# The last filter's xm in another buffer, and the Fourier stage's subtractions from GpSimd to VectorE

## The chip, the cores and the metric

The kernel runs on one core of one Trainium2 chip. A core has several engines that work side by side: TensorE (matmuls), VectorE, ScalarE, GpSimd, and SyncE (SP), which here only starts DMA transfers. Each engine takes its instructions in the order in which they were written into its own stream, and waits there where a semaphore says that an operand or a buffer isn't ready. In the rows of the profile they are called PE, DVE, ACT, POOL and SP. The metric is the device time of one execution in microseconds, as the median over runs. Lower is better.

## The reference

One encoder layer is computed for two sequences (prompt and sample) of 1024 rows by 1024 channels, in float32. Cut to what matters:

```python
xn = rmsnorm(x, g_pre)
p = xn @ w_in                                    # 1024 x 8192
fv, fg, hv, hg, mg = split(p)
fz = fftn(fv, axes=(row, within a group of 256), norm="ortho").real
y_f = (fz * silu(fg)) @ w_fourier_out
v, x1, x2 = split(short_conv(hv, w_short))       # width 3, each channel
kf = hyena_filters(...)                          # 2 x 1024 filters, as spectra
z = v
for n, gate in enumerate((x1, x2)):
    z = gate * (irfft(rfft(z, 2L) * kf[:, n])[:L] + hyena_d[n] * z)
y_h = (z * silu(hg)) @ w_hyena_out
g_f, g_h = split(sigmoid(mg + b_merge))
y = x + rmsnorm((g_f * y_f + g_h * y_h) @ w_out, g_post)
```

The filters depend on no input sequence, so they are made once and serve both.

## The kernel before, in words

Every float32 operand of a large matmul is split into two halves, a high one (h) and a low one (l = value - h). `split` makes h on ScalarE (a cast) and l by a subtraction on the engine that its argument names. `mm3` then issues three matmuls (h·h, h·l, l·h) for each product. Names ending in h and l in the rows are these halves.

**The Fourier stage** takes about the first 245 us. The first sequence goes through `first_half`, with `two_weights` for its first weights. For the second sequence, `xtile` (L427 to L451) is called for each of eight tiles k of 128 channels. It loads `xk`, scales and transposes it on TensorE (`tpx`) into `xg`, adds and subtracts the two mirrored halves of `xg` into the even and odd part of `eo`, and splits `eo` into `eh` and `el`. `weights` (L458 to L468) does the like for a slice `wfv` of the weights: sum `wer`, difference `wor`, and their halves `we` and `wo`. The matmuls `pfv` multiply both; `pse`, `pso`, `pP` and `pQ` make the transforms behind them, and VectorE's `sst`, `pp`, `qp`, `fA` and `fB` work on those.

**The filter stage** (`phase_main`, about 245 to 700 us) makes 16 filters. `filter_taps` (L737) makes a filter's taps: matmuls `pft` from the hidden layer `hid`, an exponential `ex` on ScalarE, the products `T` and sums of their absolute values `acc` on VectorE, and then the matmul `pn`, which sums over partitions. `filter_spectrum` (L774) takes `T` and `pn`'s reciprocal `invn`, forms the sums `fE` and `fO`, from these `xp` and `xm`, and hands both to `butterfly` (L659), which leaves them in `b`, `bs`, `bh` and `bl`. `forward` turns these by the matmuls `pXf` into a spectrum, which is stored as `kt`. Between the filters stand the large projection matmuls `pin` (`inproj`), which need nothing of the filters, and so fill TensorE's time. The projection's own weights `wr` are loaded by SP, and their low half `wl` is a subtraction on GpSimd, here and in the whole kernel. The hidden layer is loaded from memory as `hidr` at the stage's start.

**The branches** (about 670 to 1667 us) begin with `conv(1, 0)`: the projection `pin`, ScalarE's scaled copy into `v` (L873), and two VectorE steps on `v` (L874, L875). `conv_front` (L896) makes `eo4` from it (written `eo` in the rows) and transposes that on TensorE (`tph`). After the branches come three output products.

**Buffers.** A tile is taken by its tag from a pool; with `bufs=1` the next tile of that tag waits until the last reader of the one before is done. `Rooms` sends a tag to one of two pools: "q", with two buffers, is in the first, and "u", with one, in the second. `xp` takes "q". `xm` takes "u", and so does `v`, which is the only output of `conv` that does.

**The order of work** isn't written out by hand. A scheduler works with its own model of times on the whole program, and sets the order in each engine's stream once, before the program runs. An edit at one place can thus move rows at others.

Of the kernel before, what the change touches and what calls it, by code (L numbers as in the profile page):

```python
# [9 lines left out]
F32 = mybir.dt.float32  # L10
# [6 lines left out]
P = 128  # L17
# [143 lines left out]
class K:  # L161
# [265 lines left out]
    def xtile(self, b, k, px, fo):  # L427


        nc, a = self.nc, self.a  # L430
        xt = px.tile([P, 8, P], F32, tag="x", name=f"xk{b}_{k}", bufs=3)
        nc.sync.dma_start(xt.rearrange("p m c -> p (m c)"), a["x1c"][k])
        xg = px.tile([P, L + 2], F32, tag="xg", name=f"xg{b}_{k}", bufs=2)
        nc.gpsimd.memset(xg[:, L:L + 2], 0.0)
        for n in range(2):
            tp = self.psum("mm", 4, "tpx")
            for q in range(4):
                m = 4 * n + q
                self.mm(tp[:, q * P:(q + 1) * P], xt[:, m], self.diag[:, m], True, True)
            nc.scalar.activation(xg[:, 512 * n:512 * n + 512], tp, AF.Copy, scale=self.gpre[:, k:k + 1])  # L440
        nc.sync.dma_start(self.d_x[b][k], xg[:, 0:L])
        eo = px.tile([P, 2, 2, 256], F32, tag="eo", name="eo", bufs=2)
        fw = xg[:, 0:512].rearrange("p (a r) -> p r a", r=2)
        bw = xg[:, 1024:512:-1].rearrange("p (a r) -> p r a", r=2)
        self.add("dve", eo[:, 0], fw, bw)
        self.sub("pool", eo[:, 1], fw, bw)
        self.split(fo["eh"][:, k], fo["el"][:, k], eo, "dve", "act")
        x5 = fo["x5"][:, k]
        hi = x5[:, b:b + 33:32]
        nc.scalar.copy(hi, xg[:, 512:513].to_broadcast([P, 2]))  # L450
        nc.scalar.activation(x5[:, 2 + b:35 + b:32], hi.bitcast(F32), AF.Identity, bias=xg[:, 512:513], scale=-1.0)  # L451
# [6 lines left out]
    def weights(self, pw, W, half, k):  # L458

        nc, a = self.nc, self.a  # L460
        w = pw.tile([P, 2, 2, 130], F32, tag="wfv", name="wfv", bufs=2)
        nc.sync.dma_start(w.rearrange("p a b c -> p (a b c)"), a["w_fv"][k * P:(k + 1) * P, half])
        we = pw.tile([P, 2, 130], F32, tag="wer", name="wer", bufs=2)
        wo = pw.tile([P, 2, 128], F32, tag="wor", name="wor", bufs=2)
        self.add("dve", we, w[:, :, 0], w[:, :, 1])
        self.sub("pool", wo, w[:, :, 0, 0:128], w[:, :, 1, 0:128])
        for r, t in ((we, W[0]), (wo, W[1])):
            self.split(t[0][:, k], t[1][:, k], r.rearrange("p a b -> p (a b)"), "pool" if r is wo else "dve", "act")  # L468

    def mm3(self, out, L_, R_, start, stop):  # L470

# [302 lines left out]
    def filter_spectrum(self, n, ct, T, ws):  # L774
        nc = self.nc
        E = ws.tile([P, 4, 2, P], F32, tag="t4", name="fE", bufs=2)
        O = ws.tile([P, 4, 2, P], F32, tag="t4", name="fO", bufs=2)
        for h, t in enumerate(T):
            self.add("dve", E[:, 2 * h:2 * h + 2], t[:, :, 0], t[:, :, 1])
            self.sub("dve", O[:, 2 * h:2 * h + 2], t[:, :, 0], t[:, :, 1])  # L780
        xp = ws.tile([P, 2, 4, P], F32, tag="q", name="xp", bufs=2)
        xm = ws.tile([P, 2, 4, P], F32, tag="u", name="xm", bufs=1)
        self.add("dve", xp[:, 0], E[:, :, 0], E[:, ::-1, 1])
        self.sub("dve", xm[:, 0], E[:, :, 0], E[:, ::-1, 1])
        self.sub("dve", xp[:, 1], O[:, :, 0], O[:, ::-1, 1])
        self.add("dve", xm[:, 1], O[:, :, 0], O[:, ::-1, 1])
        B = self.butterfly(ws, xp, xm)
        for g, pairs in GROUPS:
            X = self.forward(g, pairs, B[g], "pXf")
            kt = ws.tile([P, 8, P], F32, tag="k", name="kt", bufs=2)  # L790
            tmp = ws.tile([P, 2, 2, P], F32, tag="tt", name="ktmp", bufs=4)
            th = lambda j: self.th[:, 6 * pairs[0] + j:6 * pairs[0] + j + 1]
            if g:

                nc.scalar.activation(tmp, X, AF.Copy, scale=th(0))
                self.stt("dve", kt[:, 0:6:5], X[:, :, 1], th(1), tmp[:, :, 0])
                self.stt("dve", kt[:, 2], X[:, 1, 0], th(4), tmp[:, 1, 1])
                self.stt("dve", kt[:, 4], X[:, 0, 0], th(1), tmp[:, 0, 1], MUL, SUB)
                self.turned = nc.scalar.mul(kt[:, 1:4:2], kt[:, 0:4:2], -1.0)
            else:  # L800
                for i, pr in enumerate(pairs):
                    R, I = X[:, i, 0], X[:, i, 1]
                    th = lambda j: self.th[:, 6 * pr + j:6 * pr + j + 1]
                    nc.scalar.activation(tmp[:, i, 0], R, AF.Copy, scale=th(0))
                    nc.scalar.activation(tmp[:, i, 1], R, AF.Copy, scale=th(3))
                    self.stt("dve", kt[:, 2 * i], I, th(1), tmp[:, i, 0])
                    self.stt("dve", kt[:, 4 + i], I, th(2), tmp[:, i, 1])
                    if i == 0:
                        t2 = ws.tile([P, P], F32, tag="y", name="kt2", bufs=1)
                        nc.scalar.activation(t2, R, AF.Copy, scale=th(4))  # L810
                        self.stt("dve", kt[:, 1], I, th(5), t2)
                    else:
                        nc.scalar.mul(kt[:, 3], kt[:, 2], -1.0)
            o = KOFF[g] * P
            dk = self.d_k[n][ct][:, o:o + 8 * P].rearrange("p (a b) -> p a b", a=8)
            nc.sync.dma_start(dk[:, 0:4], kt[:, 0:4])
            for r in range(2):
                nc.sync.dma_start(dk[:, 4 + r::2], kt[:, 4:6])
# [902 lines left out]
```

## Time and profile before

| what | value |
|---|---|
| runs | 2364.63, 2364.76, 2366.9 us, median 2364.76 |
| profiled execution, its own time | 2366.49 us |
| its span, first to last instruction | 2364.7 us |
| mean granted TensorE clock | 0.996 |
| busy: TensorE, VectorE, ScalarE, GpSimd | 2322.0, 1968.6, 1117.0, 449.8 us |

Of these 449.8 us on GpSimd, 51.4 lie in subtractions of the Fourier stage's weights and tiles. The times that follow are counted from the start of the span of the profiled execution, and so lie 1.8 us below its own time. A row of a timeline reads: start, duration, engine, line, operation, written tile <- read tiles, shapes, count, and in brackets how long the engine had stood idle, and on whom it had waited. A row of groups has the count, then busy time and mean ns of one, then the idle time before them. A row of the list of waits has total, number, and longest.

### The profile page before, as it was taken

To read this page: it belongs to the slowest core of one execution; us is meant where nothing else is said; L and a number is where in the kernel's file an instruction comes from. 1 tells how busy PE (TensorE), PEld (TensorE's weight loads), DVE (VectorE), ACT (ScalarE), POOL (GpSimd) and SP (SyncE) were. 2 spreads that over 40 slices of the span, in tenths; PEclk is the share of its full clock that TensorE was granted. 3 is DMA by queue.
4 is the path that set the end of the run, shared out by engine and by line. 5 is a ranking of instruction groups with operands and counts; after the bars stand their busy time and mean duration, and the time that the engine had idled before them with its cause. 6 is when DMAs were issued, how large, how long until landed. Compare 5 with 4: busy or idle time off the path is not lost.

```text
span 2364.7 us, 36212 instructions
## 1 busy us (share of the span) xinstructions
PE 2322.0 (98%) x12784; PEld 2019.3 (85%) x12784; DVE 1968.6 (83%) x3438; ACT 1117.0 (47%) x2080; POOL 449.8 (19%) x428
## 2 busy tenths in 40 slices
PE   6999999999999999999999999999999999999998
PEld 5999888888888888888888889888888888888787
DVE  7775688888788999999989989997765578777987
ACT  6654576777753333334222223323443364557443
POOL 3342222122223343321000000112000000101311
PEclk9999999999999999999999999999999999999999
DMA  7636765554565667667465554445854678998653
GB/s 263 210 141 215 267 211 177 180 168 155 183 219 201 194 207 216 207 198 248 165 205 167 175 171 157 159 152 194 313 167 146 218 260 269 271 312 245 199 165 142
DMA packets 246207, 479.69 MB, mean 203 GB/s; under 512 B 24582, under 2 KB 82280, under 8 KB 245706
## 3 DMA queue, kind: packets, MB, share of 16 engines
q1 hardware_dynamic: 222013, 402.25, 50.9%
q0 software_dynamic: 23792, 75.11, 11.2%
q8 instruction: 100, 1.64, 0.3%
q14 instruction: 81, 0.66, 0.1%
q10 hardware_dynamic: 221, 0.04, 0.0%
HBM read 326.82 MB, written 177.73 MB: 213 GB/s over the span
## 4 chain that ended last, share of the span: by engine, by line
PE 55%; DVE 2%; DMA 1%; ACT 1%; issue 1%; POOL 0%; DVEq 0%; POOLq 0%; ACTq 0%; SPq 0%
PE pin L194 18%; PE pg L194 15%; PE pn L194 12%; PE pT L194 5%; PE pX L194 5%; PE tph L906 1%; DMA x<-d_x 1%; DMA xr<-in_x 0%; DMA d_m<-gt 0%; DMA k<-d_k 0%; DVE x L177 0%; DVE wl L181 0%; DVE t L181 0%; DVE wraw L181 0%; ACT room L171 0%
## 5 line engine op out<-in xcount | busy, mean ns | idle before, releaser
L194 PE MATMUL pin<-x,wh 128*128 128x512 f32 x2816 | 891.5, 392 | 0.6 <-DVE x L177 0.6
L194 PEld LDWEIGHTS pin<-x,wh 128*128 128x128 f32 x2816 | 525.3, 189 | 100.7 <-ACT v L873 0.8
L194 PE MATMUL pin<-x,wl 128*128 128x512 f32 x1408 | 552.1, 392 | 0.0
L181 POOL TENSOR_TENSOR wl<-wr,wh 128x512 fp32r<-128x512 f32 x128 | 224.6, 1755 | 709.7 <-ACT wh L171 682.0
L194 PEld LDWEIGHTS pin<-x,wl 128*128 128x128 f32 x1408 | 265.6, 189 | 50.0
L194 PE MATMUL pn<-room,wh 128*128 128x512 f32 x864 | 266.1, 389 | 0.0
L194 PEld LDWEIGHTS pn<-room,wh 128*128 128x128 f32 x864 | 162.1, 188 | 33.6 <-DVE gt L181 0.2
L194 PE MATMUL pn<-room,wl 128*128 128x512 f32 x432 | 168.4, 390 | 0.1
L181 DVE TENSOR_TENSOR t<-pX,k 128x1024 f32<-128x1024 f32 x128 | 156.2, 1220 | 8.7 <-PE pX L194 7.4
L194 PE MATMUL pX<-bh,cfwd 128*128 128x256 f32 x768 | 161.3, 288 | 0.0
L194 PE MATMUL pT<-cinv,yh 128*128 128x256 f32 x768 | 145.4, 284 | 0.5 <-DVE T0s L181 0.5
L171 ACT CAST wh<-wr 128x512 fp32r<-128x512 f32 x128 | 79.3, 619 | 132.7 <-PE pin L194 96.5
L171 ACT CAST bh<-b 128x512 fp32r<-128x512 f32 x144 | 88.7, 620 | 96.2 <-DVE b L181 65.5
L1362 POOL DMA_DIRECT2D d_m<-gt x32 | 27.2, 849 | 532.8 <-DVE gt L181 505.8
L194 PEld LDWEIGHTS pT<-cinv,yh 128*128 128x128 f32 x768 | 122.8, 191 | 6.5 <-issue 0.6
L194 PEld LDWEIGHTS pX<-bh,cfwd 128*128 128x128 f32 x768 | 126.3, 190 | 2.2
L171 ACT CAST yh<-y 128x512 fp32r<-128x512 f32 x96 | 59.4, 619 | 117.7 <-DVE y L181 117.7
L194 PE MATMUL pX<-bl,cfwd 128*128 128x256 f32 x384 | 109.2, 284 | 0.0
L194 PE MATMUL pT<-cinv,yl 128*128 128x256 f32 x384 | 108.9, 284 | 0.0
L181 DVE TENSOR_TENSOR bl<-b,bh 128x512 fp32r<-128x512 f32 x144 | 101.5, 709 | 3.4 <-ACT bh L171 3.3
L1105 POOL CAST mark<-x 128x1 fp32r<-128x1 f32 x30 | 22.8, 759 | 404.2 <-DVE x L177 404.0
L907 ACT COPY xt<-tph 128x512 f32<-128x512 f32 x64 | 36.9, 587 | 128.7 <-PE tph L906 128.6
(362 smaller groups left out, 5235.8 us busy)
## 6 DMA issues: line engine op xcount, KB each, us to landing
k<-d_k SPq DMA_DIRECT2D x128, 512.0 KB, 4.2
wr<-in_w_in SPq DMA_DIRECT2D x128, 256.0 KB, 3.3
d_g<-gt SPq DMA_DIRECT2D x124, 256.0 KB, 2.9
wl<-d_s SPq DMA_DIRECT2D x56, 512.0 KB, 5.5
d_k<-kt SPq DMA_DIRECT2D x128, 128.0 KB, 2.2
d_k<-kt SPq DMA_DIRECT2D x64, 256.0 KB, 2.5
g<-d_g SPq DMA_DIRECT2D x64, 256.0 KB, 5.2
r<-d_g SPq DMA_DIRECT2D x60, 256.0 KB, 6.0
```

Of the source, the lines that this page charges most:

```text
L171: self.rounded = nc.scalar.copy(h, src)
L181: return e.tensor_tensor(out, a, b, op=op)
L194: return self.nc.tensor.matmul(out, lhsT, rhs, start=start, stop=stop, skip_group_check=shared)
L906: nc.tensor.transpose(tp[:, q * P:(q + 1) * P], eo[:, e, q], self.ident)
L907: nc.scalar.copy(xt[:, e].rearrange("p a b -> p (a b)"), tp)
L1105: with tc.issue_after(nc.gpsimd.tensor_copy(mark, z[:, 0:1]).ins):
L1362: nc.gpsimd.dma_start(dst, t, accum_op=ADD)
```

## The change

There are two parts. In `filter_spectrum`, `xm` of the last filter (n = 1, ct = 7) is taken from tag "q", with its two buffers, and no longer from "u". In `xtile` and `weights`, three subtractions are done by VectorE and no longer by GpSimd: the odd half of `eo` (8 times 128x512), `wor` (16 times 128x256) and `wo`'s low half (16 times 128x256). Three subtractions of `two_weights` (`wo<-wos,wo`, 128x512) stay on GpSimd, as do its memsets and its DMA starts.

```diff
@@ xtile
         self.add("dve", eo[:, 0], fw, bw)
-        self.sub("pool", eo[:, 1], fw, bw)
+        self.sub("dve", eo[:, 1], fw, bw)
@@ weights
         self.add("dve", we, w[:, :, 0], w[:, :, 1])
-        self.sub("pool", wo, w[:, :, 0, 0:128], w[:, :, 1, 0:128])
+        self.sub("dve", wo, w[:, :, 0, 0:128], w[:, :, 1, 0:128])
         for r, t in ((we, W[0]), (wo, W[1])):
-            self.split(t[0][:, k], t[1][:, k], r.rearrange("p a b -> p (a b)"), "pool" if r is wo else "dve", "act")
+            self.split(t[0][:, k], t[1][:, k], r.rearrange("p a b -> p (a b)"), "dve", "act")
@@ filter_spectrum
-        xm = ws.tile([P, 2, 4, P], F32, tag="u", name="xm", bufs=1)
+        last = (n, ct) == (1, 7)
+        xm = ws.tile([P, 2, 4, P], F32, tag="q" if last else "u", name="xm", bufs=1 + last)
```

The scheduler's order differs from the start up to about 720 us; behind that TensorE's order is the same. Lines behind L782 are one higher in the changed kernel.

**The last filter.** TensorE before, from the end of the matmuls of the filter ahead of it to the last filter's first `pXf` (`b_8083` is the last filter's):

```order
L194 MATMUL pXf<-bh,cfwd 128x256
L194 MATMUL pin<-x_5_3072,wh 128x512 x2
L194 MATMUL pin<-x_5_3072,wl 128x512
L194 MATMUL pin<-x_6_3080,wh 128x512 x2
L194 MATMUL pin<-x_6_3080,wl 128x512
L194 MATMUL pin<-x_7_3088,wh 128x512 x2
L194 MATMUL pin<-x_7_3088,wl 128x512
L194 MATMUL pXf<-b_8083,cfw_3092 128x128 x2
```

And the end of the same stretch in the changed kernel (`eo_8413` is made from `v`):

```order
L194 MATMUL pin<-x_2_2976,wh 128x512 x2
L907 MATMUL tph<-ident,eo_8413 128x128 x8
L194 MATMUL pin<-x_2_2976,wl 128x512
L194 MATMUL pin<-x_3_2984,wh 128x512 x2
L194 MATMUL pin<-x_3_2984,wl 128x512
L194 MATMUL pin<-x_4_3060,wh 128x512 x2
L194 MATMUL pin<-x_4_3060,wl 128x512
L194 MATMUL pin<-x_5_3068,wh 128x512 x2
L194 MATMUL pXf<-b_8083,cfw_3092 128x128 x4
```

Before, 9 `pin` matmuls stand between the two groups of `pXf`, and the transposes of `v` come after the whole filter. Now it is 52 `pin` matmuls, and the transposes come ahead of the filter's `pXf`. From the last filter's `pn` to its first `pXf` there were 24 `pin` matmuls and are 53; ahead of that `pn`, back to the `pXf` of filter 14, there were 13 and are 27.

VectorE at the same place, in one piece of the difference (`v_8409` and `eo4_8413` are the first branch's `v` and its `eo`, `xp_8076`, `bs_8082` and `b02_8083` are the last filter's):

```order
+L177 SCALAR_TENSOR_TENSOR kt_7902<-pXf_7889,th_68,ktmp_7903 128x128 x2
 L181 TENSOR_TENSOR xp_8076<-fO_8071 128x512
 L181 TENSOR_TENSOR xm_8077<-fO_8071 128x512
 L181 TENSOR_TENSOR b02_8083<-xp_8076 128x256
+L177 SCALAR_TENSOR_TENSOR kt_7925<-pXf_7912,th_68,ktmp_7926 128x2x128
+L177 SCALAR_TENSOR_TENSOR kt_7925<-pXf_7912,th_68,ktmp_7926 128x128 x2
+L181 TENSOR_TENSOR eo4_8413<-v_8409 128x512 x2
 L181 TENSOR_TENSOR b02_8083<-xp_8076 128x128 x2
 L181 TENSOR_TENSOR bs_8082<-xp_8076 128x512
```

`eo` from `v`, and `kt` of the filter before, now stand within the last filter's chain. The `kt` rows stood in it before too, a few rows later; `eo` stood after it. The two steps on `v` itself stand ahead of `invn` now, and behind `b` before.

**The start of the filter stage.** SP before, where `gt` is a result of the projection that ScalarE copies, and `hidr` the hidden layer:

```order
L854 DMA wr<-in_w_in 128x512
L893 DMA d_g_0_0_124<-gt 128x512
L854 DMA wr<-in_w_in 128x512
L893 DMA d_g_5_1_141<-gt 128x512
L1000 DMA hidr<-d_h 64x2x512 x2
L729 DMA w_2994<-in_filt_w 64x256
```

And in the changed kernel:

```order
L894 DMA d_g_0_0_124<-gt 128x512 x2
L855 DMA wr<-in_w_in 128x512 x2
L1001 DMA hidr<-d_h 64x2x512 x2
L729 DMA w_2994<-in_filt_w 64x256
L730 DMA w_2994<-in_filt_w 64x256
L732 DMA dec<-in_filt_decay 128x256
L761 DMA db<-in_hyena_d 128x128
L894 DMA d_g_5_1_141<-gt 128x512 x2
```

The store of `gt` into `d_g_5_1` stood ahead of `hidr` and stands now behind the five loads for the first filter.

**The tiles of the Fourier stage.** VectorE before:

```order
L181 TENSOR_TENSOR eo<-xg_2_1778 128x512
L547 COPY sst<-sst 128x1
L181 TENSOR_TENSOR el<-eo,eh 128x1024
L181 TENSOR_TENSOR eo<-xg_3_1802 128x512
L177 SCALAR_TENSOR_TENSOR fA<-pQ,vec,fPs 128x258
```

And in the changed kernel:

```order
L181 TENSOR_TENSOR eo<-xg_2_1778 128x512 x2
L181 TENSOR_TENSOR sst<-sev,pso 34x258
L181 TENSOR_TENSOR sst<-sev,pso 34x255
L547 COPY sst<-sst 34x1
L181 TENSOR_TENSOR eo<-xg_3_1802 128x512 x2
L181 TENSOR_TENSOR el<-eo,eh 128x1024
```

Each tile now has two `eo` rows on VectorE, and the work on `sst` and `fA` stands elsewhere between the tiles.

## The prediction

> **What bounds the kernel now.** I read the page first, then the list of TensorE's waits, then a table of stretches, and last the timeline around each place named there.
>
> ```profile
> PE 2322.0 (98%) x12784; PEld 2019.3 (85%) x12784; DVE 1968.6 (83%) x3438; ACT 1117.0 (47%) x2080; POOL 449.8 (19%) x428
> PE pXf L194 <- ACT bs L691: 2.7, 1, 2.7
> PE pn L766 <- DVE acc L181: 2.1, 1, 2.1
> PE pQ L194 <- DVE fB L177: 1.8, 3, 0.7
> ```
>
> TensorE is busy in 98% of the span, so an edit that leaves its matmuls alone can give back only its halts. The change removes no matmul. The two longest halts that lie near edited code are the 2.7 (pXf, the last filter) and the 2.1 (pn, the first filter); the third is the longest that VectorE causes in the Fourier stage after its start.
>
> ```profile
> 42.00:104.00 62.00, 59.77 (x492) 58.24 (x491) 47.49 (x128) 36.29 (x86) 21.08 (x34) 1.00 0.63 212
> 104.00:142.00 38.00, 35.23 (x299) 34.47 (x298) 34.05 (x53) 27.46 (x60) 16.56 (x19) 1.00 0.68 244
> 142.00:240.00 98.00, 97.87 (x678) 90.61 (x677) 55.88 (x136) 43.39 (x99) 28.03 (x29) 1.00 0.46 162
> 266.00:276.00 10.00, 7.89 (x32) 6.32 (x31) 7.87 (x16) 5.29 (x12) 1.73 (x1) 0.83 0.98 345
> 676.00:692.00 16.00, 12.74 (x50) 10.70 (x49) 16.00 (x36) 9.41 (x21) 2.30 (x3) 0.68 0.51 159
> 300.00:400.00 100.00, 100.00 (x563) 87.66 (x562) 85.50 (x198) 67.79 (x148) 22.74 (x15) 1.00 0.62 198
> ```
>
> The columns are the stretch, its length, busy time of TensorE, of its weight loads, of VectorE, ScalarE and GpSimd, the granted clock, DMA share, GB/s. A usual stretch (300 to 400) loses nothing. At 266 and 676 TensorE not only stands still, its clock falls as well (0.83 and 0.68), which no busy share shows: 0.17 x 10 = 1.7 us and 0.32 x 16 = 5.1 us of full-speed work on top of the halts.
>
> **The change, part by part. 1: xm in the other buffer.** The last filter's chain in the trace of before:
>
> ```profile
> 678.47 0.39 PE L194 MATMUL pin<-x,wl 128*128 128x512 f32 x1
> 681.55 1.19 PE L194 MATMUL pXf<-b,cfw 128*128 128x128 f32 x4 [2.69 <-ACT bs L691]
> ...
> 670.10 0.28 PE L767 MATMUL pn<-ones,acc 128*128 128x2 f32 x2
> ...
> 670.41 0.17 DVE L768 RECIPROCAL invn<-pn 128x1 f32<-128x1 f32 x1 [0.60 <-PE pn L767]
> 671.96 0.60 DVE L177 SCALAR_TENSOR_TENSOR kt<-pXf,th,ktmp 128x128 f32<-128x128 f32 x2
> 680.52 1.22 DVE L181 TENSOR_TENSOR b<-bs 128x256 f32<-128x256 f32 x2
> 684.12 0.75 DVE L181 TENSOR_TENSOR b<-xm,bs 128x256 f32<-128x256 f32 x2
> 687.10 1.28 DVE L177 SCALAR_TENSOR_TENSOR v<-pin,wsh,v 128x1023 f32<-128x1023 f32 x1
> 691.77 1.29 DVE L181 TENSOR_TENSOR eo<-v 128x512 f32<-128x512 f32 x2
> ...
> 685.09 1.11 ACT L873 ACTIVATE v<-pin,wsh 128x1024 f32<-128x1024 f32 x1
> ```
>
> ScalarE writes v 0.2 us after the last reader of xm (684.12 + 0.75 = 684.87): v shared xm's one buffer and waited for it. From pn's end to the first pXf TensorE needs VectorE for 681.55 - 670.10 = 11.4 us, and VectorE has no pause there. TensorE's own work behind pn ends at 678.47 + 0.23 = 678.7, hence the halt of 2.7 and the fall of the clock.
>
> With v free earlier, the order is another. TensorE's rows between pn and the first pXf of the last filter grow from 24 to 53 pin matmuls, plus 8 transposes (tph). Prices:
>
> ```profile
> 1636.01 31.76 PE pin L194 x140
> ...
> 699.22 1.04 PE L906 MATMUL tph<-ident,eo 128*128 128x128 f32 x8
> ```
>
> 31.76 / 140 = 0.227 us for a pin, so 29 x 0.227 + 0.9 = 7.5 us more cover: from pn, 678.7 - 670.1 + 7.5 = 16.1. VectorE's chain gains an eo pair (1.29) and one x step (1.27, as v's row has it), and loses one kt pair (0.60), which goes ahead of invn: 11.4 + 1.29 + 1.27 - 0.6 = 13.4. The two v steps (2 x 1.28) go ahead of invn; they are paid for by the same matmuls, now ahead of pn (27 pins instead of 13 between the filter before and pn, +3.2). So pXf would be ready 2.7 us before TensorE asks. The halt and its fall go: 2.69 + 5.1 = -7.8. Ends: -8.1 (the half-covered 0.57 us wait for x in the same slow stretch goes too, at half) and 0, if the chain is 2.7 late after all. I take -7.8, because both sums are made of rows with few strangers. No queue is held by the edit: xm's new buffer had held xp of the filter before, read for the last time a filter earlier.
>
> The Trainium skill, page "TensorE: Matmul & The Clock Gate", section "HAM oscillation — how this bites in real kernels", puts the rule at idle gaps of more than about 3.4 us. By it neither 2.69 nor 2.10 us would cost clock, and the two places would give 4.8 us back and no more. The granted clock in the two stretches above says otherwise; the measurement decides.
>
> **2: the first filter's pn.** Nothing is edited there, but the order moves.
>
> ```profile
> 270.52 0.46 PE L766 MATMUL pn<-acc,ones 128*128 128x128 f32 x2 [2.10 <-DVE acc L181]
> ...
> 235.21 0.33 SPq L854 DMA_DIRECT2D wr<-in_w_in  x1
> 240.86 0.32 SPq L893 DMA_DIRECT2D d_g<-gt  x1
> 241.23 1.33 SPq L1000 DMA_DIRECT2D hidr<-d_h  x2
> ...
> 240.25 1.07 ACT L887 COPY gt<-pin 128x512 f32<-128x512 f32 x2
> 246.47 1.05 ACT L1003 CAST hid<-hidr 128x1024 fp32r<-128x1024 f32 x1 [5.14 <-DMA hidr<-d_h]
> ...
> 255.73 0.77 DVE L181 TENSOR_TENSOR sums<-sums 128x512 f32<-128x512 f32 x1 [1.74 <-DMA sums<-d_x]
> ```
>
> The chain to pn begins with hidr's load. It stands on SP behind a store of gt, which waits for ScalarE's copy (240.25), and ScalarE then waits 5.14 us for the load. In the new order hidr stands ahead of that store, behind wr (235.21), so it can go out about 5 us earlier; the cast can then start once ScalarE has done gt, at 241.3. The store comes after five more loads, 1.33 + some 3.2 us of issue by these rows' spacing; nobody reads it soon. Price: 2.10 + 1.7 = 3.8 if 2.1 or more of these 5 arrive at pn. Ends: 0 (the sums, which wait 1.74 for a load of their own, hold VectorE instead) and -3.8. I take -3.8, since sums' loads stand on SP behind a weight load that itself waits for the same chain, so they move with it. TensorE asks only 3 pins (0.7) earlier.
>
> **3: no GpSimd arithmetic in xtile and weights.** Three groups move from GpSimd to VectorE; the third row below, of two_weights, stays on GpSimd.
>
> ```profile
> L181 POOL TENSOR_TENSOR wo<-wor,wo 128x256 fp32r<-128x256 f32 x16 | 15.8, 1000 | 25.0 <-ACT wo L171 24.7
> L181 POOL TENSOR_TENSOR eo<-xg 128x512 f32<-128x512 f32 x8 | 14.1, 1765 | 11.0 <-ACT xg L440 5.3 <-DVE el L181 2.5 <-ACT x L451 1.9
> L181 POOL TENSOR_TENSOR wo<-wos,wo 128x512 fp32r<-128x512 f32 x3 | 8.5, 2817 | 3.9 <-ACT wo L171 3.9
> L181 POOL TENSOR_TENSOR wor<-wfv 128x256 f32<-128x256 f32 x16 | 13.0, 821 | 4.1 <-DMA wfv<-in_w_fv 3.8 <-DVE sst L547 0.3
> ...
> L181 DVE TENSOR_TENSOR wos<-wfv 128x256 f32<-128x256 f32 x8 | 3.4, 420 | 0.0
> ...
> L181 DVE TENSOR_TENSOR el<-eo,eh 128x1024 fp32r<-128x1024 f32 x8 | 12.3, 1550 | 0.0
> L181 DVE TENSOR_TENSOR eo<-xg 128x512 f32<-128x512 f32 x8 | 8.7, 1090 | 0.4
> ...
> 122.40 1.22 DVE L181 TENSOR_TENSOR el<-eo,eh 128x1024 fp32r<-128x1024 f32 x1
> 123.75 0.69 DVE L181 TENSOR_TENSOR eo<-xg 128x512 f32<-128x512 f32 x1
> 124.36 2.55 DVE L181 TENSOR_TENSOR el<-eo,eh 128x1024 fp32r<-128x1024 f32 x1
> ...
> 124.23 1.59 POOL L181 TENSOR_TENSOR eo<-xg 128x512 f32<-128x512 f32 x1
> ```
>
> VectorE gets 32 x 0.42 (wos is the same shape on VectorE) + 8 x 0.69 = 19.0 us. It also gets something back: el takes 1.22 alone and 2.55 when GpSimd's eo runs beside it (124.23 to 125.82). In the tile stage (104 to 142) the means above give 8 x (1.55 - 1.22) + 8 x (1.09 - 0.69) = 5.8 back against 8 x 0.69 = 5.5 more. So VectorE's 34.05 of 38 us stays as it is. From 42 to 104 it has 47.49 of 62; all 32 steps of the weights, with nothing given back, would make 60.9. From 142 to 240 it has 55.88 of 98. The cover for the 19 us is thus VectorE's own idle time and what it gets back. If it were gone, the matmuls would wait for el. GpSimd's queue keeps its memsets and stores, which come earlier if anything.
>
> Net: TensorE's halts there are 62 - 59.77 = 2.2 and 38 - 35.23 = 2.8, so -5.0 is the lower end. Upper end: one new halt like pn's with its fall of the clock, 3.8, as the 60.9 of 62 would leave room for: +4. I take -0.5, near zero, since the waits for fB (1.8) stem from VectorE's order and are as likely to move as to go.
>
> The Trainium skill, page "SBUF — State Buffer", section "Who interferes with whom", says that a VectorE operation with two SBUF inputs and a GpSimd operation that reads SBUF block each other whole, whichever starts second. By that, el at 124.36 would start its work at 125.82 and end at 127.04; it ended at 126.91, so the trace agrees, and all of the stretching would go.
>
> **Sum** against the profiled execution (span 2364.7, total 2366.49): -7.8 - 3.8 - 0.5 = -12.1, 2354.4. The median of the runs shown (2364.76) lies 1.7 below the profiled one, with one run of three as high as it; I say 2354.0.
>
> **Rivals.**
> A. pn's halt stays: the loads of sums hold the chain. For it: VectorE waits 1.74 us for sums in the midst of it. 2366.5 - 7.8 - 0.5 = 2358.2.
> B. The last filter's halt only moves. For it: VectorE is busy in 16.00 of 16 us there and now has v, eo and x ahead of b. Against: 2.7 us of reserve in the two sums. If it is eaten, pXf waits again and the clock may fall again: 2366.5 less 0 to 4, with a gain at pn or without: 2359 to 2366.
> C. The Fourier stage or the rewritten order up to 720 brings one new halt with a fall of the clock (3.8 to 7.8 by the two seen): 2354.4 + 3.8 to 7.8 = 2358 to 2362.
> D, slower: VectorE becomes the bound of the tile stage. Place: each of the eight tiles needs eo, eo, el from VectorE in order. If nothing of the stretch came back, it would have 34.05 + 5.5 = 39.6 us of work in 38, and every tile's pfv could wait. One halt like pn's costs 3.8; with the last filter's gain kept, four such halts (15.2) give 2366.5 - 7.8 + 15.2 = 2373.9, and that is the point from which it is slower than what a measurement can tell. Against: the row at 124.36 shows the stretch to be GpSimd's.
> E. The change doesn't do what it says: three subtractions of 128x512 stay on GpSimd. The stage has them in any case, so they move the sum by nothing; the title's saving on GpSimd is 42.9 of its 51.4 us there.
>
> **How the numbers follow.** The forecast (both halts gone, Fourier within 2.5) 0.44; A 0.22; C 0.12; B 0.13; D 0.09. A measurement of this kernel tells 0.2% (4.7 us) from no change: faster means below 2360.0, slower above 2369.5. Forecast and A are faster, and a half of C and a sixth of B: 0.74. Same: the rest of B and C, 0.17. Slower: D, 0.09. The range: below, Fourier's -5.0 in part, 2350; above, to the upper end of B, 2365. It leaves out D and about 0.1 beyond its edges.
>
> **What would show it.** Right: no row of pXf waiting for bs, the granted clock 1.00 from 660 to 720, v written before the last filter's invn; hidr's load issued about 236 and pn without a wait, clock 1.00 around 270; el at 1.22 each in the tiles and VectorE near 34 us there. Wrong: a wait of pXf, tph or pn of 2 us or more with the clock below 1.00 after it, or pfv waiting for el tile after tile.

## The result, and the profile after

The changed kernel takes 2355.19 us in the median of six runs (2354.23 to 2359.28), the kernel before 2364.95 (2362.66 to 2366.9). The ratio is 0.9963, with a 95% interval of 0.9952 to 0.9974: 0.37% faster, 9.8 us. Timed again on another chip it is 2354.91 to 2367.02, 0.9948 (0.9936 to 0.9960). The prediction had said 2354.0.

The profiled execution of the changed kernel took 2355.4 us, with a span of 2353.6, 11.1 less than before. That is close to its median, while the profiled execution of before (2366.49) lies 1.5 above its own, so the stretches below add up to 11.1 and not to 9.8. The rows of TensorE's waits in the changed kernel that answer to those shown of before, and the new one (total, number, longest):

```profile
PE pXf L194 <- ACT kt L814: 1.7, 1, 1.7
PE pXf L194 <- DVE b L181: 0.7, 1, 0.7
PE pn L766 <- DVE acc L181: 0.2, 1, 0.2
PE tpx L194 <- DMA xk<-in_x1c: 0.9, 1, 0.9
PE pQ L194 <- DVE qp L181: 0.6, 1, 0.6
```

The wait of 2.7 for `bs` is gone, pn's has fallen from 2.1 to 0.2, and a new one stands in the list: pXf, 1.7, for ScalarE's `kt`. The stretches of the changed kernel, with the columns as before:

```profile
42.00:104.00 62.00, 60.35 (x503) 59.30 (x502) 47.39 (x145) 38.93 (x92) 5.34 (x14) 1.00 0.63 210
104.00:142.00 38.00, 36.23 (x303) 35.32 (x303) 32.11 (x62) 26.88 (x58) 2.71 (x10) 1.00 0.62 236
142.00:240.00 98.00, 98.00 (x673) 90.73 (x671) 62.47 (x155) 45.12 (x100) 18.12 (x19) 1.00 0.50 174
290.00:310.00 20.00, 18.29 (x95) 16.02 (x95) 12.64 (x27) 11.50 (x24) 4.77 (x5) 0.91 0.94 305
676.00:692.00 16.00, 16.00 (x88) 13.78 (x87) 14.67 (x34) 9.15 (x23) 7.97 (x9) 1.00 0.48 154
```

At 676 to 692 TensorE is busy throughout, at full clock (12.74 of 16 and 0.68 before). At 290 to 310 the clock is 0.91, where before nothing was lost.

To compare stretches whose work has moved, I add up by how much each matmul starts later after the one before it than the usual distance for its width (the median of its width in the kernel before). This is TensorE's lost time, halts and slow clock together, and doesn't depend on which matmuls lie in a stretch. In us, for one profiled execution of each kernel:

| stretch (us) | before | after | after, again | xm only | Fourier only | xm, eo | xm, weights |
|---|---|---|---|---|---|---|---|
| to 42, start | 28.0 | 26.9 | 29.1 | 28.5 | 29.1 | 28.9 | 29.0 |
| 42 to 240, Fourier | 8.2 | 5.3 | 4.1 | 8.6 | 5.2 | 11.1 | 7.6 |
| 260 to 290, first pn | 4.0 | 0.6 | 0.1 | 2.5 | 0.1 | 1.6 | 0.5 |
| 290 to 400 | 0.6 | 5.4 | 1.8 | 0.9 | 4.9 | 6.0 | 3.7 |
| 400 to 640 | 2.8 | 1.2 | 1.3 | 2.8 | 1.2 | 1.2 | 1.2 |
| 640 to 700, last filter | 8.0 | 0.3 | 0.2 | 0.2 | 6.8 | 0.3 | 0.3 |
| 700 to 2150, branches and after | 3.8 | 4.4 | 4.5 | 16.7 | 4.3 | 4.5 | 4.9 |
| behind 2150 | 11.2 | 11.4 | 11.5 | 11.5 | 10.9 | 11.5 | 11.2 |
| sum | 66.6 | 55.5 | 52.7 | 71.7 | 62.6 | 65.0 | 58.3 |

The 11.1 us between the first two columns are thus 7.7 at the last filter, 3.0 in the Fourier stage, 3.4 at the first pn, 1.6 between 400 and 640 and 1.1 at the start, less 4.8 that the stretch from 290 to 400 took back and 0.8 behind 700. An execution isn't always typical of its kernel: that of xm and eo is the slowest of eleven (2364.95 us, median 2361.14), and the second one of the changed kernel the fastest of five (2352.68, median 2354.91).

### The profile page after: what moved, and what is told of

Its sections match the earlier page's. It is cut to its first block, busy times and chain, and to the rows that moved or that the text cites. A ratio compares the mean times of both kernels' runs of the same rounds, so it can differ in the third digit from the quotient of the medians.

```text
span 2353.6 us, 36191 instructions
## 1 busy us (share of the span) xinstructions
PE 2316.1 (98%) x12784; PEld 2015.2 (86%) x12784; DVE 1971.6 (84%) x3478; ACT 1108.1 (47%) x2072; POOL 421.0 (18%) x388
## 4 chain that ended last, share of the span: by engine, by line
PE 57%; DVE 2%; DMA 1%; issue 1%; ACT 0%; POOL 0%; DVEq 0%; POOLq 0%; ACTq 0%
PE pin L194 19%; PE pg L194 15%; PE pn L194 12%; PE pT L194 5%; PE pX L194 5%; PE tph L907 1%; DMA xr<-in_x 0%; DMA d_m<-gt 0%; DMA k<-d_k 0%; DVE x L177 0%; DVE t L181 0%; DVE b L181 0%; DVE wl L181 0%; DVE y L181 0%; DVE yl L181 0%
## 5 line engine op out<-in xcount | busy, mean ns | idle before, releaser
L181 POOL TENSOR_TENSOR wl<-wr,wh 128x512 fp32r<-128x512 f32 x128 | 237.8, 1858 | 717.5 <-ACT wh L171 680.1
L194 PEld LDWEIGHTS pn<-room,wl 128*128 128x128 f32 x432 | 81.1, 188 | 17.9 <-DVE wl L181 1.1
```

The lines of the kernel that those rows point to most:

```text
L181: return e.tensor_tensor(out, a, b, op=op)
L194: return self.nc.tensor.matmul(out, lhsT, rhs, start=start, stop=stop, skip_group_check=shared)
```

## The experiments

**The last filter's xm alone.** The three subtractions stay on GpSimd.

```diff
-        xm = ws.tile([P, 2, 4, P], F32, tag="u", name="xm", bufs=1)
+        last = (n, ct) == (1, 7)
+        xm = ws.tile([P, 2, 4, P], F32, tag="q" if last else "u", name="xm", bufs=1 + last)
```

> Only xm of the last filter moves to the other buffer; the three subtractions stay on GpSimd. Theory (each halt goes for its own reason): the last filter's pXf no longer waits and the granted clock there stays at 1.00, worth the 7.7 us that TensorE lost between 640 and 700 us; the first filter's pn keeps its wait of about 2.1 us and its fall of the clock, since hidr's load still stands behind the store of gt. About 2357 us against 2365. Rival (the buffer is not the cause, the new order of the whole program is): the wait for bs stays near 2.7 us and the time near 2365.

Measured: 2374.91 us to 2366.8, ratio 1.0032 (1.0020 to 1.0045), slower. This kernel's stretches:

```profile
266.00:276.00 10.00, 7.81 (x39) 6.34 (x38) 8.28 (x15) 4.76 (x11) 2.49 (x2) 1.00 1.03 345
640.00:700.00 60.00, 60.00 (x324) 51.94 (x323) 53.17 (x118) 36.26 (x79) 23.16 (x26) 1.00 0.64 209
1300.00:1320.00 20.00, 17.67 (x105) 15.35 (x104) 18.19 (x28) 6.95 (x12) 1.04 (x2) 0.91 0.61 202
1475.00:1495.00 20.00, 17.61 (x99) 15.35 (x98) 14.70 (x20) 6.89 (x11) 2.40 (x2) 0.91 0.38 127
```

At the place of the edit the theory holds: 640 to 700 is full, at full clock, and 7.8 us are won. But from 700 on 12.9 us more are lost than before, in halts that the kernel before doesn't have; behind those of the last two stretches the clock fell. Its waits of TensorE between 720 and 1667 us:

```profile
PE tph L907 <- ACT T1s L960: 2.7, 2, 2.1
PE pT L194 <- ACT yh L171: 1.5, 2, 1.2
PE pX L194 <- DVE t L181: 1.4, 1, 1.4
PE pX L194 <- DVE bl L181: 1.2, 2, 1.0
...
PE pn L766 <- DVE acc L181: 2.2, 1, 2.2
```

(The last row is of the list from 250 to 720: pn still waits, as the theory had it.) The cause of the halts in the branches lies in the order of rows. In the changed kernel TensorE's last 8467 matmuls, from about 735 us on, are those of the kernel before, one for one by tile and shape, and so they are in the eight other kernels of the layer below, none of which has these halts. With xm alone only the last 3124, from 1650 us on, are the same, and `tph`, `pT` and `pX` stand where their operands aren't ready. So neither of my two theories was right on the time: the buffer is the cause of the last filter's halt, and with the same edit the scheduler wrote the branches in a worse order. Why it settles on the good order in the one kernel and not in the other wasn't found out.

**The Fourier part alone.** The changed kernel with xm back in "u".

```diff
-        xm = ws.tile([P, 2, 4, P], F32, tag="q" if last else "u", name="xm", bufs=1 + last)
+        xm = ws.tile([P, 2, 4, P], F32, tag="u", name="xm", bufs=1)
```

> Only the three subtractions of the Fourier stage move to VectorE; xm stays in the shared buffer. Theory: the last filter's wait of 2.7 us and the clock of about 0.68 behind it stay; the Fourier stage gives 3 to 4 us back, pn's halt goes (3.4) and a new halt of the filter stage near 295 us takes 3.5 to 4.8 of it, as in the changed kernel: 2361 to 2363 us, 2358 if the new halt stays away. Rival (the Fourier part only trades one halt for another and VectorE's longer list costs what GpSimd's saves): 2365, no change.

Measured: 2362.83 to 2366.8, ratio 0.9988 (0.9979 to 0.9997). TensorE's waits from 250 to 720 us in this kernel:

```profile
PE pXf L194 <- DVE b L181: 3.8, 2, 2.0
PE pin L194 <- DVE x L177: 2.6, 1, 2.6
PE pXf L194 <- ACT kt L813: 1.5, 1, 1.5
```

pn's wait is gone, the new one for kt is there, and the last filter keeps its own: a pXf for b and a pin for x, 6.8 us lost with one fall of the clock. (The other of the two waits for b stands at 316 us, behind the one for kt.) The theory's range, 2361 to 2363, holds the time. This and the changed kernel differ in xm only, and TensorE's rows behind 720 us are the same: xm's buffer is worth 6.8 - 0.3 = 6.5 us here, by the ratios, each to the kernel before on its own chip, 0.9988 - 0.9963 = 0.25%, 5.9 us, or more by the changed kernel's second ratio, 0.9948.

**xm with eo alone, and xm with the weights alone.**

```diff
-        self.sub("dve", wo, w[:, :, 0, 0:128], w[:, :, 1, 0:128])
+        self.sub("pool", wo, w[:, :, 0, 0:128], w[:, :, 1, 0:128])
...
-            self.split(t[0][:, k], t[1][:, k], r.rearrange("p a b -> p (a b)"), "dve", "act")
+            self.split(t[0][:, k], t[1][:, k], r.rearrange("p a b -> p (a b)"), "pool" if r is wo else "dve", "act")
```

> xm, and of the subtractions eo's alone; the weights' stay on GpSimd. Theory (VectorE's stretching by GpSimd is what the Fourier stage gets back): el takes 1.22 us in the tiles as in the changed kernel, while wer and we keep means above 0.55 us; of the Fourier stage's 3 to 4 us about 1 to 2 come. hidr stands ahead of the store, so pn does not wait. 2354 to 2358 us. Rival (the gain of the Fourier stage comes from the new order of rows, not from the stretching): 2354 with the stretching of wer and we still there.

```diff
-        self.sub("dve", eo[:, 1], fw, bw)
+        self.sub("pool", eo[:, 1], fw, bw)
```

> xm, and of the subtractions the weights' alone; eo's odd half stays on GpSimd. Theory: wer and we fall to 0.42 us each, el keeps a mean near 1.5 us in the tiles and TensorE keeps most of its 3.6 us of halts between 104 and 142; pn does not wait. 2354 to 2358 us. Rival (order, not stretching): 2354 or below with el still stretched.

Measured, beside 2366.8 for the kernel before on their chip: xm and eo 2361.14, ratio 0.9977 (0.9968 to 0.9986), a smaller gain than expected; xm and the weights 2358.25, ratio 0.9964 (0.9951 to 0.9976), no different from the whole change's 0.9963. What eo's subtraction adds to the time is thus not shown. VectorE's groups of the first of the two, el and eo in the tiles (104 to 142 us), then we and wer in the whole stage:

```profile
L181 DVE TENSOR_TENSOR eo<-xg 128x512 f32<-128x512 f32 x16 | 10.2, 684 | 1.5 <-ACT xg L440 1.4
L181 DVE TENSOR_TENSOR el<-eo,eh 128x1024 fp32r<-128x1024 f32 x8 | 9.7, 1216 | 1.3 <-ACT eh L171 1.3
...
L181 DVE TENSOR_TENSOR we<-wer,we 128x260 fp32r<-128x260 f32 x16 | 9.4, 606 | 1.7 <-ACT we L171 1.6
L181 DVE TENSOR_TENSOR wer<-wfv 128x260 f32<-128x260 f32 x16 | 9.0, 569 | 2.5 <-DMA wfv<-in_w_fv 2.3
```

And of the second, in the same order:

```profile
L181 DVE TENSOR_TENSOR el<-eo,eh 128x1024 fp32r<-128x1024 f32 x8 | 10.9, 1366 | 1.1 <-ACT eh L171 1.0
L181 DVE TENSOR_TENSOR eo<-xg 128x512 f32<-128x512 f32 x8 | 10.0, 1264 | 1.5 <-ACT xg L440 1.5
...
L181 DVE TENSOR_TENSOR wer<-wfv 128x260 f32<-128x260 f32 x16 | 6.7, 426 | 2.1 <-DMA wfv<-in_w_fv 2.0
L181 DVE TENSOR_TENSOR we<-wer,we 128x260 fp32r<-128x260 f32 x16 | 6.7, 423 | 0.1
```

VectorE's stretching goes exactly where GpSimd's subtraction goes, and stays where it stays. That is shown, and it agrees with the Trainium skill's page "SBUF — State Buffer", section "Who interferes with whom", by which two such operations of VectorE and GpSimd take turns as a whole. That TensorE's gain follows it isn't: with eo on VectorE the stretch from 42 to 240 lost 11.1, more than before (a pP waited 2.1 for ScalarE at 171 us and the clock fell), with the weights there 7.6 (a fall at 126 us). Neither half alone brings the stage's 3.0 us, in the one execution profiled of each, the slowest of its runs in the first case.

**All of the stage's arithmetic on VectorE.**

```diff
-            self.split(*[p[:, 2 * kp:2 * kp + 2] for p in W[i]], r, "pool" if kp and i else "dve", "act")
+            self.split(*[p[:, 2 * kp:2 * kp + 2] for p in W[i]], r, "dve", "act")
```

> The changed kernel, and the three 128x512 subtractions of two_weights on VectorE as well, so that no arithmetic of the Fourier stage is left on GpSimd. Theory (GpSimd's subtractions stretch VectorE's rows there, but the start waits for something else): rs_t falls from a mean of 0.34 us to 0.16; the halts before 42 us (23 to 24 us) change by less than 1; the time stays within 2 us of the changed kernel, 2354 to 2358. Rival (the stretched rs_t holds the start): the start's waits shrink by 2 us or more, 2352.

Measured: 2359.03 to 2367.16, ratio 0.9970 (0.9960 to 0.9980). `rs_t<-rs_t,rs_m`, a step of rmsnorm's scale on 128x4 elements, falls from a mean of 0.34 us to 0.16, as both theories had it (two of its twelve rows took about 1.25 us beside a subtraction on GpSimd, and none does now), and the start doesn't get shorter; in the profiled execution it lost 30.4 us with 6.8 us at half clock, against 26.9 to 29.1 in the table. The three that the change leaves on GpSimd cost it nothing.

**dec's load on another queue.** `dec` holds a filter's decay rates. Its load stands on SP behind a weight load, and ScalarE waits for it ahead of the kt that the new halt near 295 us waits for. In the changed kernel:

```profile
284.61 0.33 SPq L855 DMA_DIRECT2D wr<-in_w_in  x1
...
285.51 0.38 SPq L732 DMA_DIRECT2D dec<-in_filt_decay  x1
...
290.18 0.42 ACT L734 ACTIVATE dec<-dec 128x256 f32<-128x256 f32 x1 [2.61 <-DMA dec<-in_filt_decay]
...
292.16 1.71 ACT L754 ACTIVATE ex<-dec,vec 128x256 f32<-128x256 f32 x4
...
296.58 0.31 ACT L814 ACTIVATE kt<-kt 128x128 f32<-128x128 f32 x1 [0.42 <-DVE kt L177]
...
296.95 0.35 PE L194 MATMUL pXf<-bh,cfwd 128*128 128x256 f32 x1 [1.71 <-ACT kt L814]
```

The load was moved to ScalarE's queue, then to GpSimd's:

```diff
-        nc.sync.dma_start(dec, a["filt_decay"][n, ct].partition_broadcast(P))
+        nc.scalar.dma_start(dec, a["filt_decay"][n, ct].partition_broadcast(P))
```

> The changed kernel, with the load of dec issued by ScalarE and not by SP, where it stood behind a weight load that waits for GpSimd. Theory (the new halt near 295 us comes from dec's late landing, which holds ScalarE for 2.6 us and with it kt and the matmuls pXf): ScalarE's wait for dec goes, pXf's wait of 1.7 us and the fall of the clock behind it go; 3.5 to 4.8 us less than the changed kernel, about 2351. Rival (ScalarE has too much to do there in any case, the exponentials and the table loads are what holds kt): a halt of 1 us or more stays between 290 and 320, 2354 to 2357.

> The changed kernel, with dec's loads issued by GpSimd and not by SP (the third queue after SP and ScalarE). Theory (the start of the filter stage is bound by one chain through VectorE and ScalarE, whose lack shows at pn or at the pXf behind it, whatever the queue): the stretch from 260 to 400 loses 4 us or more, as with dec on SP (6.0) and on ScalarE (4.8); the time within 2 us of the changed kernel. Rival (dec's queue is the cause): under 2 us lost from 260 to 400, 2351.

On ScalarE's queue: 2355.69 to 2367.16, ratio 0.9957 (0.9941 to 0.9974). The stretches:

```profile
260.00:280.00 20.00, 17.74 (x79) 14.46 (x79) 15.63 (x29) 10.30 (x21) 5.38 (x4) 0.91 0.97 338
290.00:320.00 30.00, 30.00 (x169) 26.29 (x169) 27.06 (x60) 19.93 (x47) 9.39 (x8) 1.00 0.83 268
```

The halt at 295 is gone, as the theory had it, and pn's is back, 2.3 us with a fall, so the theory's gain of 3.5 didn't come. On GpSimd's queue: 2354.07 to 2367.02, ratio 0.9949 (0.9935 to 0.9963). There pn waits 1.0 and pXf 0.8, no fall follows, and 260 to 400 loses 2.8 us, between the theory's 4 and its rival's 2. Neither is faster than the changed kernel beyond the intervals.

**hidr's load on another queue, in the kernel before.**

```diff
-                nc.sync.dma_start(hid[64 * i:64 * i + 64].rearrange("p (n t) -> p n t", n=2),
+                nc.gpsimd.dma_start(hid[64 * i:64 * i + 64].rearrange("p (n t) -> p n t", n=2),
```

> The kernel before, with hidr's load issued by GpSimd and not by SP, where it stood behind the store of gt; nothing else is edited. Theory (pn's halt comes from hidr's late load): hid's cast comes 3 us or more earlier, pn waits less than 0.5 us and the clock there stays at 1.00: 3.4 to 3.8 us less than the kernel before, if no new halt takes it back; by what the changed kernel showed, a halt of about 1.7 us with a fall of the clock may come behind it at about 295, and then the time is the kernel before's. Rival (the loads of sums or the table loads hold the chain): pn still waits 1.5 us or more.

Measured: 2369.32 to 2367.16, ratio 1.0012 (1.0003 to 1.0022). This run didn't do what it was for. On GpSimd the load stood behind a weight subtraction and went out later than before, at 242.61, and hid's cast came at 251.93, not 3 us earlier but 5.5 later. pn waits 0.5 all the same, because the scheduler had put 16 more matmuls ahead of it, and behind it 290 to 400 loses 3.7. It decides nothing on hidr, and a better test follows.

**The store ahead of hidr on another queue, in the kernel before.**

```diff
-            nc.sync.dma_start(self.d_g[b][sec][ct][:, s], t)
+            (nc.scalar if (b, sec, ct) == (0, 5, 1) else nc.sync).dma_start(self.d_g[b][sec][ct][:, s], t)
```

> The kernel before, with the two stores of gt (branch 5, tile 1) that stand ahead of hidr's load issued by ScalarE, so that hidr's load has only the weight load ahead of it on SP. TensorE's rows are the kernel before's but for some 200 around the first two filters. Theory (pn waits because hidr's load stands behind that store): the load goes out 5 us earlier, at about 236, hid's cast at about 242, pn waits under 0.5 us with the clock at 1.00, and 260 to 290 loses 0.5 and not 4.0. The time is 3 to 3.5 us less than the kernel before's if the next filter has room, or its own within 1.5 us if a halt comes behind it between 290 and 400, as it did in one execution of the changed kernel. Rival (the loads of sums, or ScalarE's exponentials, hold the chain): pn waits 1.5 us or more although the cast comes earlier.

Measured: 2363.86 to 2366.11, ratio 0.9991 (0.9981 to 1.0000). The load on SP, the cast on ScalarE, and the stretch at pn:

```profile
234.21 1.34 SPq L1000 DMA_DIRECT2D hidr<-d_h  x2
...
240.40 1.05 ACT L1003 CAST hid<-hidr 128x1024 fp32r<-128x1024 f32 x1 [0.46 <-ACT gt L887]
...
266.00:276.00 10.00, 10.00 (x53) 8.59 (x52) 7.34 (x14) 4.54 (x10) 2.47 (x2) 1.00 0.99 349
```

The load goes out 7 us earlier and the cast comes 6.1 earlier, held now by gt's copy alone. The chain ahead of pn ends at 265.42, 5 us earlier, and TensorE has only 4 more matmuls ahead of it. pn has no wait left, and 260 to 290 loses 0.1 and not 4.0; 290 to 400 loses 1.8 and not 0.6. So pn waited for the store ahead of hidr: the theory is right, and the rival falls. The time is 2.2 us less by the medians, with an interval from nothing to 4.5, which holds the theory's 3 to 3.5. (The execution profiled here is the fastest of its eleven.)

**The changed kernel again.**

> The changed kernel once more, unaltered, beside the kernel before on this chip, to see which of its halts come again. Expected: the last filter's stretch (640 to 700 us) loses under 0.5 us, the Fourier stage between 42 and 240 loses 5 to 6.5, the start of the filter stage (260 to 320) 4 to 6, all within 1 us of the first profile save for single falls of the clock of 1.7; the time 0.36% below the kernel before. Rival (the halt near 295 was one execution's): 260 to 320 loses under 2.

Measured: ratio 0.9948, the Fourier stage loses 4.1, less than expected, and the last filter 0.2. At 295 the same rows in the same order now wait 0.3 us and lose 0.8 from 290 to 320, without a fall; ScalarE waited 1.38 us for dec and not 2.61. That the halt was one execution's, as the rival has it, isn't so, though. TensorE's rows are the changed kernel's there in three other kernels: with the Fourier part alone, with the weights, and with all arithmetic on VectorE. In these pXf waited 1.5, 0.9 and 1.4 us for kt, and 4.5, 2.6 and 4.7 us were lost from 290 to 320. So four of five executions of this order have a halt of 0.9 us or more there, and the fifth was the fastest run of its kernel. This execution's stretch, and its row:

```profile
290.00:310.00 20.00, 19.71 (x108) 17.04 (x107) 16.25 (x36) 12.05 (x25) 5.29 (x6) 1.00 1.03 339
...
296.10 0.35 PE L194 MATMUL pXf<-bh,cfwd 128*128 128x256 f32 x1 [0.29 <-ACT kt L814]
```

**What a halt costs the clock.** A kernel without the layer's work: TensorE runs blocks of matmuls, and waits between two for a chain of VectorE operations. Cut to what matters:

```python
for i, (k, h) in enumerate(HALTS):        # 43 halts, 11 lengths
    for m in range(n):                    # 160, then 53 to 70
        nc.tensor.matmul(ps, lhs, r, start=m == 0, stop=m == n - 1)
    # a chain of 1 to 7 VectorE operations from ps to the next r
```

> All the kernel's work is left out; its outputs hold zeros. TensorE runs dense blocks of 53 to 70 matmuls of 512 columns, and between two blocks waits for a chain of VectorE operations of set length, from about 0.7 to 4.2 us, each length four times. Theory (a halt of about 2 us is enough to halve the granted clock for at least 3.4 us, but not always): no fall behind halts under 1.5 us, falls behind some of those of 1.7 to 3 us, behind nearly all of those above 3.4. Rival (the Trainium skill's page on TensorE: only gaps above about 3.4 us count): no fall behind any halt under 3.2 us.

By the starts of the matmuls and the trace's records of the clock:

| halt (us) | 0.9 to 1.0 | 1.7 | 2.1 | 2.4 | 2.9 | 3.1 | 3.6 | 3.9 | 4.3 to 5.0 |
|---|---|---|---|---|---|---|---|---|---|
| halts | 4 | 4 | 4 | 4 | 4 | 4 | 4 | 4 | 11 |
| clock fell behind | 0 | 0 | 1 | 2 | 3 | 3 | 3 | 4 | 11 |

Two halts of one length, 2.1 us by the starts (the brackets leave the last matmul's end out), and the clock in the 14 us around each:

```profile
282.70 1.67 PE L1717 MATMUL ps<-r,lhs 128*128 128x512 f32 x6 [1.97 <-DVE r L1731]
680.49 3.13 PE L1717 MATMUL ps<-r,lhs 128*128 128x512 f32 x8 [1.97 <-DVE r L1731]
...
276.00:290.00 14.00, 12.03 (x53) 9.59 (x53) 1.81 (x3) 0.00 (x0) 0.00 (x0) 1.00 0.00 1
676.00:690.00 14.00, 12.03 (x47) 9.46 (x46) 1.81 (x3) 0.00 (x0) 0.00 (x0) 0.88 0.00 0
```

The theory holds: in this one execution no halt of 1.7 us or less cost clock, and of those from 2.1 to 3.6 some did. What decides is where a halt lies: all falls begin on one grid of 3.413 us, and last one or two of its steps. Taking the idle time that falls into one step of the grid, all 26 halts with 2.13 us or more in a step were followed by a fall, and none of the 14 with 1.72 or less; of three between 1.89 and 1.97 one was. The Trainium skill's page "TensorE: Matmul & The Clock Gate" names this window of about 3.4 us, which runs freely, in its section "What's actually happening", and there this run agrees. That a whole window must be idle, as it also says, doesn't: some 2 us of it are enough.

The layer's kernels show the same grid. I add up TensorE's idle time in each step between 42 and 2330 us of their twelve traces. All 12 steps that began at full clock and held 1.71 us or more were followed by a fall, two of the five between 1.54 and 1.68 were, and none with less. So short halts in one step add up: with dec's load on ScalarE's queue the clock fell at 2181 us behind halts of 0.48 and 1.06. And with xm alone pn's 2.19 us lay across two steps, 1.68 in one, and no fall came. The fall at the last filter before lasted three steps, 10.24 us; TensorE waited again within it, 0.57 us for x.

## Why the prediction was right, point by point

**Part 1, xm's buffer: right in mechanism, and in size for this execution.** Forecast -7.8, measured -7.7 (8.0 to 0.3; 7.8 and 6.5 by the two kernels that isolate it). That the two agree so well has luck in it: both take the halt's price from one execution of the kernel before. The three other kernels that keep xm in "u" lost 6.8, 7.6 and 6.0 there. The chain's rows in the changed kernel:

```profile
665.83 0.28 PE L767 MATMUL pn<-ones,acc 128*128 128x2 f32 x2
681.90 1.05 PE L194 MATMUL pXf<-b,cfw 128*128 128x128 f32 x8
...
662.69 1.28 DVE L177 SCALAR_TENSOR_TENSOR v<-pin,wsh,v 128x1023 f32<-128x1023 f32 x1 [0.31 <-ACT v L874]
666.15 0.17 DVE L768 RECIPROCAL invn<-pn 128x1 f32<-128x1 f32 x1 [0.47 <-PE pn L767]
678.24 0.75 DVE L181 TENSOR_TENSOR b<-bs 128x256 f32<-128x256 f32 x2
```

b is done 13.2 us behind pn (forecast 13.4), TensorE asks for it after 16.1 (forecast 16.1), and the reserve is 2.9 (forecast 2.7). v stands ahead of invn and delays it by nothing: VectorE still waits 0.47 for pn. Rival B didn't come about.

**The clock's fall.** The 5.1 us were in this sum as if they belonged to the halt. They came and went with it, but a halt of this length can stay without one: with xm alone, pn waited 2.2 us with the clock at 1.00 (first stretch shown there), where the kernel before fell behind 2.1, all of it in one step of the grid. At the last filter the fall also hid a second wait: the kernel with the Fourier part alone, and the one with hidr on GpSimd's queue, keep the halt, have a shorter fall, and wait 2.6 us more for x or bh a few us later. So the halt's price there was probably in part VectorE's work showing in another way; no run tests that by itself.

**Part 2, the first pn: right where it looked, and short by one step.** Forecast -3.8, measured -3.4 (4.0 to 0.6), and the cause as stated: hidr's load goes out at 232.16 and not at 241.23, 9 us earlier (forecast about 5), and the cast comes 9.4 earlier. The row of SP in the changed kernel, and of ScalarE:

```profile
232.16 1.35 SPq L1001 DMA_DIRECT2D hidr<-d_h  x2
...
237.11 1.06 ACT L1004 CAST hid<-hidr 128x1024 fp32r<-128x1024 f32 x1
```

The step that failed is the one that ended the chain at pn. Behind it the same filter's last pXf waits for kt, which stands on ScalarE behind dec's load and four exponentials; in this execution that cost 4.8 us from 290 to 400, more than pn gave. Rival C had priced such a halt at 3.8 to 7.8 with a chance of 0.12, but as something added anywhere, not as the gain at pn handed back. In the second execution the stretch lost 1.2 more than before and most of the gain stayed, but as shown above the halt is the rule for this order and not the exception. The run with the store on another queue shows pn's cause by itself; those with dec's load on another queue show that the halt behind it can be had at pn, at pXf, or in parts at both.

**Part 3, the Fourier stage: the mechanism right, the size too small.** VectorE's 34.05 us in the tiles were to stay "near 34": 32.11 and, again, 33.04; el at 1.22 as forecast. The sum's -0.5 was mis-sized: measured -3.0 and -4.1, within its lower end of -5.0. I had left the halts in place because they stemmed from VectorE's order; they did, and the order changed: no wait for fB is left in the list. But the stage varies from execution to execution. With the rows of before TensorE lost 8.2, 8.6, 7.3 and 5.4 us there (before, xm alone, hidr's queue, gt's store), with those of the changed kernel 5.3, 4.1, 5.2, 4.8 and 3.8 (its two executions, the Fourier part alone, dec's two queues): 7.4 and 4.6 in the mean, so that some 2.8 us are the edit's. VectorE took on 19.0 us of work by the forecast's prices, and from 42 to 240 it was busy only 4.6 longer (142.0 and 137.4, the sums of the rows shown): the rest came back, from 42 to 104 too (47.39 us, where the forecast's bound was 60.9). Whether TensorE gains by that or by the new order of rows stays open, since neither half of the edit showed the gain. Rival D had no part: VectorE's eight el in the tiles took 12.3 us beside GpSimd and 9.8 without it.

**The sum.** -7.7 - 3.4 - 3.0 + 4.8 - 1.8 (the rest) = -11.1 against the forecast's -12.1. Two terms missed by 2.5 and 4.8 in opposite ways, so the total looks better than its parts. The rest holds the start's -1.1, which isn't the change's: in the ten other executions the start is longer than before's. It also holds -1.6 between 400 and 640, which is the change's and which no term had: every kernel with a part of the Fourier edit lost 1.2 or 1.3 there, the four without it 2.7 to 3.1.

## What to carry to other kernels

Two tiles that share one buffer tie two chains that have nothing else in common; look for the writer that starts right behind the other tile's last reader (here 0.2 us), and give one of them a buffer that is idle there. A gain at a halt is safe only when the next chain on the same engines has room: follow the released work to the next wait before adding the two up. Where a scheduler sets the order, an edit is worth what its order is worth: the same line won 7.8 us at its place and lost 12.9 half a kernel later.

## What the runs showed of the hardware

The granted clock falls on a fixed grid of 3.413 us, behind some 2 us of idle time within one step (1.54 to 1.71 in the layer's traces, 1.9 to 2.13 in the kernel of halts), so a halt of one length costs 1.7 us more in one place and not in another. GpSimd's subtractions stretch VectorE's operations beside them: el takes 1.22 us in the mean of its eight turns without one and 1.55 with it, and a tiny operation on 128x4 elements goes from 0.34 to 0.16 us in the mean once the last of these subtractions has left the stage.
